# The selected-keys mixer: lower weight halves on another engine, and scaling ahead of maxima

## The chip, the cores and the metric

The kernel runs as one program on one core of one Trainium2 chip. The metric is the device time of one execution in microseconds; lower is better. The engines are named as in the profile: PE (TensorE matmul), PEld (its weight loads), DVE (VectorE), ACT (ScalarE), POOL (GpSimd) and SP (SyncE, which issues the weight loads).

## The reference, cut to what matters

Four layers run one after the other on 256 rows of width 1024: two of a first block (convolutions, attention, experts) and two of a second. The change touches one place, the mixer of the last layer (`_nsa`). It has 16 heads in 4 groups that share keys and values. Each head attends three times: to 15 compressed keys, to selected keys, and to a window of keys. At 256 rows the selection holds every earlier block and the window every earlier key, so both are causal attention over all keys, with different key projections:

```python
def _masked_softmax(s, mask):
    s = jnp.where(mask, s.astype(F32), -jnp.inf)
    m = jnp.max(s, axis=-1, keepdims=True)
    e = jnp.exp(s - m)
    l = jnp.sum(e, axis=-1, keepdims=True)
    p = e / jnp.where(l > 0, l, 1.0)

# selected keys, and the same with kw, vw for the window:
s = jnp.einsum('bghqd,bgqkd->bghqk', qc, kk) * ATTN_SCALE + bias
pr, _ = _masked_softmax(s, (dist >= 0)[:, :, None])
out = jnp.einsum('bghqk,bgqkd->bghqd', pr, vv)
# o = gate0 * o_cmp + gate1 * o_slc + gate2 * o_win, then o @ w_out
```

## The kernel before

**Weights.** Every dense product is made of three matmuls (`mm3`, L397 to L399) from a weight's higher and lower part. A weight tile of 1 MB has two halves of 128x1024. ACT rounds a half to its higher part (`wh`, L237). The lower part is the difference (`wl`, L248), made on DVE, or on POOL while the switch `on_pool` is set. `half()` and `tick()` do this up to three halves ahead of the matmuls. In the mixer `nsa_mix` the switch is set before the last two query units and cleared in the sixth tick of the output product.

**Attention by pairs.** Two heads with one kind of keys make a `Pair`; there are 16, four for each group: selected (0, 1), window (2, 3) and so on. A pair goes through these parts, and the words here are used below for pair n:
- scores(n): PE multiplies queries by keys (`two_heads`, L1375), each head into a bank of its own. For selected keys DVE also adds the bias of the compressed keys (L1790, "mask additions"). For the first window pair of a group DVE subtracts the compressed minima (L1819 to L1821), for the second it normalises the compressed weights (L1829 to L1837).
- M(n), maxima: four DVE instructions add the bias and take the extreme of each row (L1409). They read the banks of the scores, which are free after that.
- E(n): four exponentials on ACT with row sums (L1414).
- S(n), scaling: DVE inverts the sums, multiplies by the gate and scales the rows (L1419, L1421, four times L1424).
- T(n): PE turns the rows (L1431, six transposes into two banks) and ACT evicts them (`pT`, L1432).
- V(n): PE multiplies by the values (L1442, L1444). After a window pair ACT and DVE split the result for the output product (`yh`, L1447, and `yl`, L1448).

**Order.** Nothing is scheduled: each engine takes its instructions in the order in which the code is written. `step()` number i runs scores(i) and M(i) with E(i), then S(i-1), T(i-2), V(i-3) (L1770). Steps 0 and 1 lie in the two value units; step 1 falls into the matmuls of the third query unit. Steps 2, 3 and 4 follow closely, step 5 stands inside the fourth query unit, steps 6 to 10 follow closely again, and steps 11 to 18 are called one by one in the ticks of the output product `feat_out`, between groups of 24 weight matmuls. A query unit also has a norm: ACT squares (L1338), DVE reduces (L1340 to L1342), POOL takes a power (L1344), DVE scales (L1348, L1350), PE turns, and ACT and DVE write the result (L1365, L1366). PSUM has eight banks; `feat_out` holds four of them, and scores, transposes and values share the rest.

Of the kernel before, what the change touches and what calls it, by code (L numbers as in the profile page):

```python
# [70 lines left out]
def tile_kernel(ctx: ExitStack, tc: tile.TileContext, A, out, first=0, last=9):  # L71
# [120 lines left out]
    def pump(n=1000):  # L192
        while loaded[0] < len(items) and n:
            i = loaded[0]
            p = next((p for p in free if usable(p, i)), None)
            if p is None:
                return
            free.remove(p)
            t = pools[p].tile([128, 2048], F32, name="w", tag="w")
            v = items[i]  # L200
            a, b = v.shape[1], v.shape[2]
            Q.dma_start(t[:, :a * b].rearrange("p (a b) -> p a b", a=a), v)
            raw[i], where[i] = t, p
            loaded[0] += 1
            n -= 1
# [19 lines left out]
    on_pool = [False]  # L225
# [45 lines left out]
    def later(n, f):  # L271
        heapq.heappush(due, (now[0] + n, now[1], f))
        now[1] += 1
# [127 lines left out]
    def feat_unit(xh, xl, opening=False):  # L401

        ps = bank()
        for m in range(2):
            h, l = half()
            if opening and not m:
                for a, b in ((h, xh), (l, xh), (h, xl)):
                    for k in range(8):
                        T.matmul(ps[:, 0:256], a[:, k, :], b[:, k, :], start=a is h and b is xh and k == 0,
                                 stop=b is xl and k == 7)  # L410
                tick()
                continue
            for k in range(8):
                mm3(ps[:, m * 256:(m + 1) * 256], h[:, k, :], l[:, k, :], xh[:, k, :], xl[:, k, :], k == 0, k == 7)
            tick()
        return ps
# [889 lines left out]
    def feat_out(yh, yl, nxt):  # L1306

        pss = [bank() for _ in range(4)]

        def part(u, h, l, c0, ks):  # L1310
            for m in range(2):
                q = slice(c0 + m * 128, c0 + m * 128 + 128)
                for i, k in enumerate(ks):
                    mm3(pss[u][:, m * 256:(m + 1) * 256], h[:, i, q], l[:, i, q], yh[:, k, :], yl[:, k, :],
                        k == 0 and m == 0, k == 7, skip_group_check=True)
                if not m:
                    middle()
        for k in range(0, 8, 2):
            if k == 6:
                drain()  # L1320
            for j in range(2):
                h, l = half()
                for u in (2 * j, 2 * j + 1):
                    part(u, h, l, (u % 2) * 256, (k, k + 1))
                    if k == 6:
                        add_unit(u, pss[u], nxt)
                        if u == 2:
                            split_high(limit(here[0] + 2))
                if k < 6:
                    tick()  # L1330
        nxt(4)
# [61 lines left out]
    class Pair:  # L1393
# [6 lines left out]
            self.gate, self.values = gate, values  # L1400

        def a(self):
            banks = self.scores()
            m = sm.tile([128, 2, 2], F32, name="sM", bufs=3)
            l = self.l = sm.tile([128, 2, 2], F32, name="sL", bufs=3)
            s = self.s = self.pool.tile([128, 2, 384], F32, name="sS", bufs=3)
            for r in range(2):
                for c, (a, n) in enumerate(PARTS):
                    V.tensor_tensor_reduce(out=s[:, r, a:a + n], in0=banks[r][:, self.starts[c]:self.starts[c] + n],  # L1409
                                           in1=self.biases[r][:, 0:n], scale=1.0, scalar=3e38, op0=OP.add,  # L1410
                                           op1=OP.min, accum_out=m[:, r, c:c + 1])
            for r in range(2):
                for c, (a, n) in enumerate(PARTS):
                    S.activation(s[:, r, a:a + n], s[:, r, a:a + n], AF.Exp, scale=-1.0, bias=m[:, r, c:c + 1],  # L1414
                                 accum_out=l[:, r, c:c + 1])
# [210 lines left out]
    def nsa_mix(bp, sl, cur, nxt):  # L1626
        with tc.tile_pool(name="ns", bufs=1, reuse_waits="tile") as cp, \
# [138 lines left out]
            def step():  # L1766

                i = step.n
                step.n += 1
                for j, f in ((i, "a"), (i - 1, "b"), (i - 2, "c"), (i - 3, "d")):  # L1770
                    if 0 <= j < len(steps):
                        getattr(steps[j], f)()
            step.n = 0
# [93 lines left out]
            for j in range(2):  # L1867
                vals.append(scaled_values(cp, tok_unit(xh, xl), cur.r, f"val{j}"))
                later(1, step)
            on_pool[0] = True  # L1870
            for g in (2, 3):
                qs, turn_q = q_unit(g)
                step()
                step()
                plan(g, bias_of(g))
                qs()
                step()
                turn_q()
                if g == 2:
                    later(1, step)  # L1880
# [2 lines left out]
            nx = nxt()  # L1883
            for j in range(1, 9):
                later(j, step)
            later(6, lambda: on_pool.__setitem__(0, False))
            feat_out(yh, yl, nx.put)
            return nx

# [17 lines left out]
    def second_block():  # L1907
        nonlocal jdent, sm
        with tc.tile_pool(name="b2", bufs=1, reuse_waits="tile") as bp, tc.tile_pool(name="sm2", bufs=2) as sm:
# [32 lines left out]
            for i, base in ((0, 5), (1, 8)):  # L1942
                if base == 8 and s0 <= 7 <= last:
                    cur = nsa_mix(bp, sl, cur, nxt(7))
                if s0 <= base + 1 and last >= base:
                    with tc.tile_pool(name="ff", bufs=1, reuse_waits="tile") as cp, \
                            tc.tile_pool(name="ffw", bufs=2, reuse_waits="tile") as cw:
                        pl = Ple(cp, i) if last > base else None
                        if s0 <= base:
                            on_pool[0] = False  # L1950
                            cur = ffn(cp, cw, i, cur, nxt(base), [(12, pl.turn)] if pl else [])
                        else:
                            pl.turn()
                        if pl:
                            cur2 = []

                            def nx1():
                                cur2.append(nxt(base + 1)())
                                return cur2[0].put
                            ple(cp, cw, pl, cur, nx1)  # L1960
                            cur = cur2[0]
# [3 lines left out]
    if 7 in stage_half:  # L1965
        j = halves[stage_half[7]][0]
# [51 lines left out]
```

## Time and profile before

| what | value |
|---|---|
| median of 3 runs | 1919.6 us (1918.84 to 1921.35) |
| the profiled execution | 1918.91 us |
| its span in the trace | 1917.3 us |
| PE, PEld busy | 85%, 64% |
| DVE, ACT, POOL busy | 39%, 35%, 6% |
| selected-keys mixer, steps 0 to 18 | about 1585 to 1683 us of the span |

Busy shares are means over stages with different limits. Most of the span is spent on the experts' weights; the mixer in question is some 100 us of it, with POOL splits at L248 among its rows. A time in the rows is counted from the span's start, and "idle before <-" names what the engine waited for last.

### The profile page before, as it was taken

What the parts mean: (1) busy time and instruction counts of PE and PEld (TensorE: products, weight loads), DVE (VectorE), ACT (ScalarE), POOL (GpSimd) and SP (SyncE); (2) the same over time, 40 slices, a digit from 0 to 9 for tenths busy, and PEclk for the clock granted to TensorE, in tenths of its full rate; (3) what the DMA queues carried; (4) which work ended last, traced back from release to release, by engine and by line L of the source; (5) the groups of instructions that cost most, each with busy time, mean ns of one, the idle gap of its engine ahead of it and who ended that gap; (6) DMA issues with size and microseconds to landing.
All of it is one profiled execution on the core that took longest, in us unless ns stands there. A gap on an engine that the chain in (4) does not pass through costs nothing. (4 is left out here: it accounts for less than half of the span.)

```text
span 1917.3 us, 35268 instructions
## 1 busy us (share of the span) xinstructions
PE 1631.0 (85%) x15117; PEld 1228.9 (64%) x15117; DVE 738.6 (39%) x1503; ACT 676.8 (35%) x1297; POOL 122.0 (6%) x126
## 2 busy tenths in 40 slices
PE   8999667677679998767667669999999998999998
PEld 7875323233238985323224227999999996799998
DVE  5551000001005661001001005666656857666557
ACT  4422111111116643111111114655444645654445
POOL 0010000000001000000000002101000412210002
PEclk9999878777789999878778789999999998999999
DMA  9689999999999469999999998545555463145550
GB/s 295 239 306 416 419 418 418 420 419 418 417 406 360 162 257 396 418 419 419 418 419 419 417 419 272 173 138 172 190 194 177 143 202 100 56 156 196 183 176 23
DMA packets 236571, 559.07 MB, mean 292 GB/s; under 512 B 15563, under 2 KB 124938, under 8 KB 236408
## 3 DMA queue, kind: packets, MB, share of 16 engines
q1 hardware_dynamic: 226520, 551.59, 75.2%
q10 hardware_dynamic: 9264, 4.97, 0.9%
q8 instruction: 122, 2.00, 0.4%
q14 instruction: 41, 0.34, 0.0%
q0 software_dynamic: 624, 0.18, 0.0%
HBM read 555.55 MB, written 1.15 MB: 290 GB/s over the span
## 5 line engine op out<-in xcount | busy, mean ns | idle before, releaser
L904 PE MATMUL ps<-w,xg 128*32 128x256 f32 x4096 | 365.0, 496 | 233.3 <-DMA w<-in_expert_w_up_dram 232.1
L904 PEld LDWEIGHTS ps<-w,xg 128*32 128x32 f32 x4096 | 136.1, 132 | 444.2 <-DMA w<-in_expert_w_up_dram 264.1
L248 DVE TENSOR_TENSOR wl<-w,wh 128x1024 fp32r<-128x1024 f32 x255 | 310.1, 1228 | 171.6 <-ACT wh L237 167.4
L237 ACT ACTIVATE wh<-w 128x1024 fp32r<-128x1024 f32 x273 | 283.1, 1051 | 91.5 <-PE ps L398 60.3
L908 DVE TENSOR_TENSOR hs<-hs,ps 128x128 f32<-128x128 f32 x64 | 18.4, 288 | 632.4 <-ACT hs L907 632.4
L397 PE MATMUL ps<-xh,wh 128*128 128x256 f32 (+1 forms) x840 | 237.1, 282 | 0.0
L399 PE MATMUL ps<-xh,wl 128*128 128x256 f32 (+1 forms) x840 | 236.3, 281 | 0.8 <-DVE wl L248 0.8
L398 PE MATMUL ps<-xl,wh 128*128 128x256 f32 (+1 forms) x840 | 236.6, 282 | 0.3 <-DVE xl L1229 0.3
L907 ACT ACTIVATE hs<-ps 128x128 f32<-128x128 f32 x64 | 17.8, 277 | 591.8 <-PE ps L904 587.2
L399 PEld LDWEIGHTS ps<-xh,wl 128*128 128x128 f32 (+1 forms) x840 | 159.2, 190 | 1.2 <-DVE wl L248 1.2
L398 PEld LDWEIGHTS ps<-xl,wh 128*128 128x128 f32 (+1 forms) x840 | 159.2, 190 | 1.1 <-DVE xl L1229 1.1
L397 PEld LDWEIGHTS ps<-xh,wh 128*128 128x128 f32 (+1 forms) x840 | 159.3, 190 | 0.0
L926 PE MATMUL ps<-w,ht 128*32 128x256 f32 x2048 | 142.2, 425 | 0.4 <-DMA w<-in_expert_w_down_dram 0.4
L933 ACT ACTIVATE y<-ps 32x256 f32<-32x256 f32 x256 | 95.8, 374 | 118.5 <-PE ps L926 111.6
L926 PEld LDWEIGHTS ps<-w,ht 128*32 128x32 f32 x2048 | 73.6, 127 | 67.6 <-issue 33.9
L399 PE MATMUL ps<-wh,xl 128*128 128x256 f32 x352 | 100.9, 287 | 4.5 <-DVE xl L1229 4.5
L397 PE MATMUL ps<-wh,xh 128*128 128x256 f32 x352 | 103.1, 293 | 1.5 <-ACT xh L1226 1.5
L248 POOL TENSOR_TENSOR wl<-w,wh 128x1024 fp32r<-128x1024 f32 x18 | 43.4, 2416 | 942.3 <-ACT wh L237 463.4
L398 PE MATMUL ps<-wl,xh 128*128 128x256 f32 x352 | 100.6, 286 | 0.0
L398 PE MATMUL ps<-al,wh 128*128 128x256 f32 x352 | 99.1, 281 | 0.0
L397 PE MATMUL ps<-ah,wh 128*128 128x256 f32 x352 | 99.1, 281 | 0.0
L399 PE MATMUL ps<-ah,wl 128*128 128x256 f32 x352 | 99.0, 281 | 0.0
(400 smaller groups left out, 2756.3 us busy)
## 6 DMA issues: line engine op xcount, KB each, us to landing
w<-in_expert_w_up_dram SPq DMA_DIRECT2D x256, 1024.0 KB
w<-in_expert_w_down_dram SPq DMA_DIRECT2D x128, 1024.0 KB
w<-in_w_ffn_gate_dram SPq DMA_DIRECT2D x22, 1024.0 KB
w<-in_w_ffn_up_dram SPq DMA_DIRECT2D x22, 1024.0 KB
w<-in_w_ffn_down_dram SPq DMA_DIRECT2D x22, 1024.0 KB
w<-in_odd_w_qkv_dram SPq DMA_DIRECT2D x12, 1024.0 KB
w<-in_w_in_ab_dram SPq DMA_DIRECT2D x12, 1024.0 KB
w<-in_w_in_nsa_dram SPq DMA_DIRECT2D x10, 1024.0 KB
```

The costliest lines, as they stand in the source:

```text
L237: S.activation(hv, src, AF.Copy)
L248: eng.tensor_tensor(out=lv, in0=src, in1=hv.bitcast(F32), op=OP.subtract)
L397: T.matmul(ps, lh, rh, start=start, stop=False, **kw)
L398: T.matmul(ps, lh, rl, start=False, stop=False, **kw)
L399: T.matmul(ps, ll, rh, start=False, stop=stop, **kw)
L904: T.matmul(pu[32 * j:32 * j + 32, 0:256], r, w[:, kk, :, j, :], start=k == 0, stop=k == 7)
L907: S.activation(hs, pu[:, 0:128], AF.Silu)
L908: V.tensor_tensor(out=hs, in0=hs, in1=pu[:, 128:256], op=OP.mult)
L926: T.matmul(pd[32 * c:32 * c + 32, 0:256], hts[e][:, 32 * j:32 * j + 32], w[:, jj, c * 256:(c + 1) * 256], start=j == 0, stop=j == 3)
L933: S.activation(y4s[q][32 * ee:32 * ee + 32, c * 256:(c + 1) * 256], pd[32 * c:32 * c + 32, 0:256], AF.Copy)
```

## The change

Two things are changed. `on_pool` is no longer set in `nsa_mix`, so that the nine lower halves that POOL made there are made on DVE, at the place in DVE's order at which the code asks for them. And `Pair.a` is cut in two, scores (`a0`) and maxima with exponentials (`a1`); `step()` now runs scores(i), S(i-1), M(i) with E(i), T(i-2), V(i-3). The other mixer that uses `Pair` calls `a`, which runs both parts at once as before.

```diff
         def a(self):
-            banks = self.scores()
+            self.a0()
+            self.a1()
+
+        def a0(self):
+            self.banks = self.scores()
+
+        def a1(self):
+            banks = self.banks
             m = sm.tile([128, 2, 2], F32, name="sM", bufs=3)
...
                 i = step.n
                 step.n += 1
-                for j, f in ((i, "a"), (i - 1, "b"), (i - 2, "c"), (i - 3, "d")):
+                for j, f in ((i, "a0"), (i - 1, "b"), (i, "a1"), (i - 2, "c"), (i - 3, "d")):
...
-            on_pool[0] = True
             for g in (2, 3):
...
-            later(6, lambda: on_pool.__setitem__(0, False))
             feat_out(yh, yl, nx.put)
```

On PE, ACT and SP every instruction keeps its place. DVE's order between M(10) and M(11), the last closely following steps, was this (sS_14238 belongs to pair 9; the next row is the first of M(11)):

```order
L1419 RECIPROCAL sL_14237<-sL_14237 128x4
L1421 TENSOR_TENSOR sL_14237<-sL_14237,gate_12972 128x4
L1424 TENSOR_SCALAR sS_14238<-sS_14238,sL_14237 128x128
L1424 TENSOR_SCALAR sS_14238<-sS_14238,sL_14237 128x256
L1424 TENSOR_SCALAR sS_14238<-sS_14238,sL_14237 128x128
L1424 TENSOR_SCALAR sS_14238<-sS_14238,sL_14237 128x256
L1448 TENSOR_TENSOR yl_12967<-ps_14211,yh_12966 128x256
L1829 TENSOR_REDUCE cl_14350<-scm_14180 128x8
L1830 TENSOR_SCALAR cl_14350<-cl_14350 128x8
L1831 RECIPROCAL cl_14350<-cl_14350 128x8
L1833 TENSOR_TENSOR cl_14350<-cl_14350,gate_12972 128x4 x2
L1837 TENSOR_TENSOR pc0_12973<-scm_14180,cl_14350 128x4x16 x2
```

and is now, again up to the first row of M(11) (sS_14291 belongs to pair 10; lines are 7 higher):

```order
L1455 TENSOR_TENSOR yl_12967<-ps_14211,yh_12966 128x256
L1836 TENSOR_REDUCE cl_14350<-scm_14180 128x8
L1837 TENSOR_SCALAR cl_14350<-cl_14350 128x8
L1838 RECIPROCAL cl_14350<-cl_14350 128x8
L1840 TENSOR_TENSOR cl_14350<-cl_14350,gate_12972 128x4 x2
L1844 TENSOR_TENSOR pc0_12973<-scm_14180,cl_14350 128x4x16 x2
L1426 RECIPROCAL sL_14290<-sL_14290 128x4
L1428 TENSOR_TENSOR sL_14290<-sL_14290,gate_12972 128x4
L1431 TENSOR_SCALAR sS_14291<-sS_14291,sL_14290 128x128
L1431 TENSOR_SCALAR sS_14291<-sS_14291,sL_14290 128x256
L1431 TENSOR_SCALAR sS_14291<-sS_14291,sL_14290 128x128
L1431 TENSOR_SCALAR sS_14291<-sS_14291,sL_14290 128x256
```

The scaling that stands between two blocks of maxima was that of pair 9, directly behind M(10); it is now that of pair 10, at the end, directly ahead of M(11).

DVE between M(11) and M(12), in the output product, before (the first row ends M(11), the last begins M(12)):

```order
L1409 ISA sM_14364 128x1
L1419 RECIPROCAL sL_14284<-sL_14284 128x4
L1421 TENSOR_TENSOR sL_14284<-sL_14284,gate_12972 128x4
L1424 TENSOR_SCALAR sS_14285<-sS_14285,sL_14284 128x128
L1424 TENSOR_SCALAR sS_14285<-sS_14285,sL_14284 128x256
L1424 TENSOR_SCALAR sS_14285<-sS_14285,sL_14284 128x128
L1424 TENSOR_SCALAR sS_14285<-sS_14285,sL_14284 128x256
L1790 TENSOR_TENSOR scm_14433<-ps_14427,cb_12968 128x32
L1790 TENSOR_TENSOR scm_14433<-ps_14428,cb_12968 128x32
L1409 ISA sS_14438,sM_14436<-ps_14427,bias_14168 128x128
```

and now:

```order
L1416 ISA sM_14370 128x1
L248 TENSOR_TENSOR wl_14398<-w_13334,wh_14397 128x1024
L1797 TENSOR_TENSOR scm_14433<-ps_14427,cb_12968 128x32
L1797 TENSOR_TENSOR scm_14433<-ps_14428,cb_12968 128x32
L1426 RECIPROCAL sL_14371<-sL_14371 128x4
L1428 TENSOR_TENSOR sL_14371<-sL_14371,gate_12972 128x4
L1431 TENSOR_SCALAR sS_14372<-sS_14372,sL_14371 128x128
L1431 TENSOR_SCALAR sS_14372<-sS_14372,sL_14371 128x256
L1431 TENSOR_SCALAR sS_14372<-sS_14372,sL_14371 128x128
L1431 TENSOR_SCALAR sS_14372<-sS_14372,sL_14371 128x256
L1416 ISA sS_14444,sM_14442<-ps_14427,bias_14168 128x128
```

A lower half came to stand between the two blocks, and the scaling (of pair 11, no longer of pair 10) behind the mask additions.

## Rows read from the trace of the kernel before

**Rows 1.** A stretch: us; busy of PE, PEld, DVE, ACT, POOL (instructions); granted clock; DMA
```profile
1626.00:1632.20 6.20, 6.10 (x28) 4.18 (x28) 5.28 (x28) 4.00 (x15) 0.00 (x0) 0.50 0.08 21
```

**Rows 2.** PE's waits from 1584 to 1692 us: total us, times, longest
```profile
PE ps L1431 <- DVE sS L1424: 8.4, 3, 5.3
PE ps L1431 <- DVE sM L1409: 1.9, 3, 1.0
```

**Rows 3.** ACT's waits in the same stretch
```profile
ACT sS L1414 <- DVE sM L1409: 22.7, 12, 3.4
```

**Rows 4.** Timeline of DVE, start and duration in us: M(2), S(1), normalising, M(3)
```profile
1601.50 0.28 DVE L1409 CUSTOM_DVE_ANT_0 sS<-ps,bias 128x128 f32<-128x128 f32 x1
...
1602.61 0.17 DVE L1419 RECIPROCAL sL<-sL 128x4 f32<-128x4 f32 x1
...
1603.94 0.28 DVE L1829 TENSOR_REDUCE cl<-scm 128x8 f32<-128x128 f32 x1
...
1605.17 0.28 DVE L1409 CUSTOM_DVE_ANT_0 sS<-ps,bias 128x128 f32<-128x128 f32 x1
```

**Rows 5.** Groups of DVE by shape, 1500 to 1700 us: busy, mean ns, idle before
```profile
L248 DVE TENSOR_TENSOR wl<-w,wh 128x1024 fp32r<-128x1024 f32 x26 | 31.7, 1231 | 15.8 <-ACT wh L237 12.6 <-POOL ssum L1242 3.1
```

**Rows 6.** Timeline of DVE, M(10) to M(11)
```profile
1641.06 0.28 DVE L1409 CUSTOM_DVE_ANT_0 sS<-ps,bias 128x128 f32<-128x128 f32 x1
...
1644.30 0.42 DVE L1448 TENSOR_TENSOR yl<-ps,yh 128x256 fp32r<-128x256 f32 x1 [0.71 <-ACT yh L1447]
...
1645.86 0.28 DVE L1409 CUSTOM_DVE_ANT_0 sS<-ps,bias 128x128 f32<-128x128 f32 x1
```

**Rows 7.** Timeline of ACT behind E(10)
```profile
1643.16 0.84 ACT L1432 ACTIVATE pT<-ps 128x384 f32<-128x384 f32 x2
1643.90 0.36 ACT L1447 ACTIVATE yh<-ps 128x256 fp32r<-128x256 f32 x1
```

**Rows 8.** Timeline of POOL: lower halves
```profile
1618.85 4.67 POOL L248 TENSOR_TENSOR wl<-w,wh 128x1024 fp32r<-128x1024 f32 x2 [16.27 <-ACT wh L237]
...
1669.46 2.39 POOL L248 TENSOR_TENSOR wl<-w,wh 128x1024 fp32r<-128x1024 f32 x1 [4.34 <-ACT wh L237]
```

**Rows 9.** Timeline of DVE: L1342 once, L1833 at two times
```profile
1621.27 2.28 DVE L1342 TENSOR_SCALAR hss<-hss 128x8 f32<-128x8 f32 x1
...
1628.52 0.24 DVE L1833 TENSOR_TENSOR cl<-cl,gate 128x4 f32<-128x4 f32 x2
...
1669.56 2.38 DVE L1833 TENSOR_TENSOR cl<-cl,gate 128x4 f32<-128x4 f32 x2
```

**Rows 10.** Timeline of DVE: M(5), the norm's reduction, M(6), M(7), M(8)
```profile
1614.61 0.28 DVE L1409 CUSTOM_DVE_ANT_0 sS<-ps,bias 128x128 f32<-128x128 f32 x1
...
1620.23 0.69 DVE L1340 TENSOR_REDUCE hss<-hsq 128x8 f32<-128x512 f32 x1 [1.95 <-ACT hsq L1338]
...
1624.18 0.28 DVE L1409 CUSTOM_DVE_ANT_0 sS<-ps,bias 128x128 f32<-128x128 f32 x1
...
1628.99 0.28 DVE L1409 CUSTOM_DVE_ANT_0 sS<-ps,bias 128x128 f32<-128x128 f32 x1
...
1632.53 0.28 DVE L1409 CUSTOM_DVE_ANT_0 sS<-ps,bias 128x128 f32<-128x128 f32 x1
```

**Rows 11.** Timeline of ACT: two higher halves ahead of the norm's square
```profile
1617.71 2.00 ACT L237 ACTIVATE wh<-w 128x1024 fp32r<-128x1024 f32 x2
```

**Rows 12.** DVE in the output product: mask additions, M(12), M(13), M(14), M(15)
```profile
1650.71 0.32 DVE L1790 TENSOR_TENSOR scm<-ps,cb 128x32 f32<-128x32 f32 x2 [2.32 <-PE ps L1375]
1650.94 0.28 DVE L1409 CUSTOM_DVE_ANT_0 sS<-ps,bias 128x128 f32<-128x128 f32 x1
...
1658.04 0.28 DVE L1409 CUSTOM_DVE_ANT_0 sS<-ps,bias 128x128 f32<-128x128 f32 x1
...
1665.22 0.29 DVE L1409 CUSTOM_DVE_ANT_0 sS<-ps,bias 128x128 f32<-128x128 f32 x1 [2.33 <-PE ps L1375]
...
1672.49 0.29 DVE L1409 CUSTOM_DVE_ANT_0 sS<-ps,bias 128x128 f32<-128x128 f32 x1 [0.22 <-PE ps L1375]
```

## The prediction

> **What bounds the kernel now.** I read the stretches first, then the waits of PE and ACT in the mixer, then the timelines of DVE, ACT and POOL there. Outside the mixer nothing moves. In it PE waits almost only for the transposes: 8.4 us for scaled rows and 1.9 us for maxima, whose end frees the banks that the transposes write [rows 2]. ACT waits 22.7 us, in 12 pieces, for maxima [rows 3]. So where steps follow closely, neither PE nor a busy engine sets the pace, but a loop between DVE and ACT. It can be read whole between M(10) and M(11) [rows 6, 7]: M(10) starts at 1641.06, the exponentials hold ACT until 1643.16, the two evictions until 1643.90, the split of the last result ends at 1644.26, DVE takes it up at 1644.30 and then normalises, and M(11) starts at 1645.86. That is 4.80 us, and in it the scaling S(9), which stands right behind M(10), costs nothing: DVE would wait anyway, and still sits idle 0.71 us behind it [rows 6]. DVE's own prices stand between M(2) and M(3) [rows 4]: maxima 1602.61 - 1601.50 = 1.11 us, scaling 1603.94 - 1602.61 = 1.33 us, normalising 1.23 us. The exponentials end some 2.2 us after their maxima start (1641.06 to 1643.16, and a tenth for the last sum).
>
> **The change: scaling ahead of maxima.** M(i) now stands behind S(i-1), which needs all sums of E(i-1). The loop therefore becomes maxima, exponentials, whatever DVE has ahead of the scaling, scaling, maxima. The 1.33 us that lay beside ACT's work move onto the loop, unless DVE has at least 2.2 - 1.11 = 1.1 us of work of its own that needs nothing late from ACT. I go step by step.
> - M(2) to M(3) has the normalising (1.23 us), so 1.11 + 1.23 + 1.33 = 3.67 us both ways [rows 4]: 0. M(7) to M(8) was 1632.53 - 1628.99 = 3.54 us [rows 10], so that the query norm's scaling and the mask additions in it take 1.1 us beside maxima and scaling; they just fill the gap, and I take +0.05, for M(3) to M(4) too.
> - M(6) to M(7), M(9) to M(10) and M(10) to M(11) have an instruction in front of the scaling that waits for the `yh` that ACT makes behind the exponentials and evictions; M(8) to M(9) has the write of turned queries, which waits for ACT in the same place. All four are the loop of rows 6 and 7 and pay in full: 4 x 1.33 = +5.3.
> - Up to M(6): M(1) and M(5) come behind mask additions that wait for PE and then pay 1.33 us each, but idle time of DVE ahead of M(5) takes the first of them back. I put M(5) at +1.4, with 0 to +2.7 as its bounds.
>
> Together M(11) starts 1.4 + 0.1 + 5.3 = 6.8 us later. The early S has no reader that gains: T(n) writes a bank that M(n+1) must have read, so transposes wait for both blocks, 2.44 us in either order.
>
> **The change: lower halves on DVE.** Nine halves of 2.4 us leave POOL [rows 8] and nine of 1.23 us come to DVE [rows 5], 11 us of work on an engine that is idle part of the time. Four of them stand in two pairs ahead of a query norm. In the second of these, M(5) to M(6), the norm's reduction started at 1620.23, when ACT had finished two higher halves (from 1617.71) and the square [rows 10, 11]. Now the first lower half can begin at about 1618.75 and the second ends at 1621.1: the reduction moves 0.85 us back. But POOL's pair no longer runs beside it, and L1342, an instruction over 8 elements a row that took 2.28 us under it [rows 8, 9], gives some 2.1 back (L1833, of a like size, lost 2.38 - 0.24 = 2.14). With the 1.33 us of S(5) that is +0.85 - 2.1 + 1.33 = +0.1, so M(6) keeps the +1.4.
>
> The other five come in the ticks of the output product. Each waits for its higher half, which ACT makes behind exponentials, evictions and the split of a result; behind it on DVE stand mask additions, scaling and maxima, and behind these maxima wait E on ACT and, for the bank, T on PE.
> - M(11) to M(12) was 1650.94 - 1645.86 = 5.08 us [rows 6, 12]. Now: exponentials 2.1, evictions 0.74, higher half 1.0 [rows 11], lower half 1.23 [rows 5], mask additions 1650.94 - 1650.71 = 0.23, scaling 1.33, in all 6.63: +1.6. PE comes no earlier, for it waits for M(11) and for the evictions too.
> - M(12) to M(13), 7.10 us [rows 12], is PE's path: transposes behind M(12), values, 24 weight matmuls, scores. It stays, but scaling now lies between the mask additions and the maxima: +1.3.
> - M(13) to M(14), 7.18 us: the loop with a split (0.36 [rows 7]), a higher and a lower half, the minima (an estimate of 0.7, between the mask additions and the normalising) and scaling adds up to about 7.5, and PE may add to it with the values that the split waits for: +0.6, with 0.3 as its lower bound. The 2.33 us that DVE was idle there [rows 12] are used up.
> - M(14) to M(15), 7.27 us, with the normalising in it and without the 2.1 us that L1833 lost under POOL [rows 8, 9]: 2.1 + 0.74 + 0.36 + 1.0 + 1.23 + 1.23 + 1.33 = 8.0, +0.7.
> - Behind M(15) a group of weight matmuls covers E(15) and S(15); without that cover they would cost 1.3.
>
> Sum: 6.8 + 1.6 + 1.3 + 0.6 + 0.7 = +11.0 us. What POOL's power instruction gains by standing alone is covered by M(2) and M(3). SP's order and the weights' loads are as before; no wait of PE in the mixer is for a load.
>
> **The clock.** Behind PE's two longest waits (most of the 8.4 us) the granted clock is 0.50, 1.2 GHz, as in the 6.2 us behind the second of them [rows 1]. It cost little, since the loop and not PE set the pace: M(6) to M(7), most of it at 0.50, took 1628.99 - 1624.18 = 4.81 us [rows 10], as long as M(10) to M(11) at full clock. Such a stretch of about 6 us over weight matmuls would cost 3. PE will wait more, also in the output product: I take +1; if both stretches go, it is at best -1, with two more of them over weight matmuls +6.
>
> The profiled execution took 1918.91 us, so +12 gives 1930.9. The median of the runs shown is 0.7 higher: **1931.5**.
>
> **The rivals.**
> - *The blocked instructions decide, and it gets faster.* The two long waits of PE are for S(1) and S(5), each behind a norm in which DVE stood blocked 2.1 us beside POOL [rows 2, 9]. If the two lower halves hide under ACT's higher halves, and scaling first lets the transposes go earlier, PE gains 2 x 2.1 = 4.2: 1915.4, some us less if the low clock goes too. The Trainium skill, SBUF — State Buffer, section Who interferes with whom, backs the blocking: a VectorE instruction with two SBUF inputs and a GpSimd instruction that reads SBUF exclude each other for a whole instruction. For L1833 the trace agrees, 2.38 us for two against 0.24 [rows 9]; by that page alone the change could only gain. It decides as soon as M(i) has more than 1.33 us of slack, and 22.7 us of ACT's waiting for maxima [rows 3] say that it has none.
> - *The output product absorbs the delay.* DVE's idle times ahead of M(12) and M(14), 2.32 and 2.33 us [rows 12], swallow part of the 6.8 us, and only the bank waits of T(10) and T(11) grow by 1.3 each: about +5, 1924.6. Against it: these idle times are waits for PE, and PE is late with the rest.
> - *The clock.* If PE's new waits bring two more stretches at 0.50 over weight matmuls, it is +6 in place of +1: 1936.5 and more.
> - *Nothing shows.* All is hidden, the change is then within 0.2%: 1919.6. It needs slack in steps 6 to 11, where rows 6 show none.
>
> **How the numbers follow.** Chances: the forecast 0.60 (alone 1927 to 1936), faster by the blocking 0.08, absorbed 0.14, clock 0.11, nothing 0.07. The range of 8 in 10 runs from 1923.5 to 1937.5; it leaves out the faster case, no change, and half of the clock's. Within 0.2% (3.8 us, about what a measurement of this kernel can tell from no change) lie the case of nothing and a little of the absorbed one, 0.09; slower 0.83; faster 0.08.
>
> **What would show it.** In the trace of the changed kernel, M(6) to M(7) and M(10) to M(11) should be about 6.1 us apart, M(7) to M(8) still 3.6, M(11) to M(12) about 6.6. PE's waits on the transposes should be for maxima, no longer for scaled rows; L1342 and L1833 should be short throughout; and the mixer should end 11 to 12 us later. The forecast is wrong if those distances stay at 4.8 us, if PE's waits shrink, or if the distances grow as said and the end does not move.

## The result and the profile after

The changed kernel takes 1936.2 us (median of 4 runs, 1934.46 to 1936.96) beside 1920.1 us of the kernel before on the same chip: a ratio of 1.0078 [1.0066, 1.009], 16 us slower. Five further runs on another occasion gave 1936.1 us and 1.0077 [1.0064, 1.0091]. The forecast was 1931.5 us in a range of 1923.5 to 1937.5: the direction and the mechanism held, and the size came out 4.7 us too small, 1.3 us inside the upper end of the range.

The profiled execution took 1936.68 us, 17.8 more than the one of before. By the starts of the maxima, 2.5 us of that stand ahead of M(0) (1588.67 against 1586.20), 15.8 between M(0) and M(15), and 0.5 us are won back behind. What is ahead of M(0) is scatter: the code is the same there, and in the executions of the experiments below M(0) starts anywhere between 1586.8 and 1591.9, the latest in kernels that are fast. So the change costs 15.8 us inside the mixer, and this is what has to be explained. Lines of the changed kernel have numbers 7 higher there: maxima L1416, exponentials L1421, scaling L1426, L1428 and L1431, transposes L1438, evictions L1439.

The waits in the changed kernel from 1584 to 1708 us (what waits and for whom; total us, times, longest), to be read against [rows 2, 3]:

```profile
ACT sS L1421 <- DVE sM L1416: 38.2, 15, 5.1
...
PE ps L1438 <- DVE sM L1416: 10.0, 7, 3.3
...
PE ps L1438 <- DVE sS L1431: 4.1, 1, 4.1
```

TensorE's transposes now wait 10.0 us for maxima, where it was 1.9, and 4.1 us for scaled rows, where it was 8.4; that one piece is T(1), behind the first norm. ACT waits 38.2 us for maxima instead of 22.7: the 15.5 us more are nearly the whole loss.

The timeline of DVE in the changed kernel, first of each group of four maxima, M(6) to M(8) and M(10), M(11), to be read against [rows 6, 10]:

```profile
1629.62 0.28 DVE L1416 CUSTOM_DVE_ANT_0 sS<-ps,bias 128x128 f32<-128x128 f32 x1
...
1635.75 0.28 DVE L1416 CUSTOM_DVE_ANT_0 sS<-ps,bias 128x128 f32<-128x128 f32 x1
...
1639.31 0.29 DVE L1416 CUSTOM_DVE_ANT_0 sS<-ps,bias 128x128 f32<-128x128 f32 x1
...
1650.50 0.28 DVE L1416 CUSTOM_DVE_ANT_0 sS<-ps,bias 128x128 f32<-128x128 f32 x1
...
1653.73 0.42 DVE L1455 TENSOR_TENSOR yl<-ps,yh 128x256 fp32r<-128x256 f32 x1 [2.04 <-ACT yh L1454]
...
1655.71 1.01 DVE L1431 TENSOR_SCALAR sS<-sS,sL 128x128 f32<-128x128 f32 x4
1656.63 0.28 DVE L1416 CUSTOM_DVE_ANT_0 sS<-ps,bias 128x128 f32<-128x128 f32 x1
```

M(6) to M(7) is 6.13 us (4.81 before), M(10) to M(11) 6.13 (4.80), M(7) to M(8) 3.56 (3.54). Between M(10) and M(11) the idle time of DVE ahead of `yl` has grown from 0.71 us [rows 6] to 2.04, by the 1.33 us of scaling that were done there, and the scaling stands behind it, right ahead of M(11). The last run of weight matmuls of the mixer starts at 1700.96 us, where it was 1682.67: 18.3 us later with the 2.5 us ahead of M(0), and so 15.8 by the mixer, not 11 to 12.

The two instructions that were held beside POOL are short now, as is seen in the second norm and in the output product (DVE, same view), to be read against [rows 9]:

```profile
1624.29 2.36 DVE L248 TENSOR_TENSOR wl<-w,wh 128x1024 fp32r<-128x1024 f32 x2 [0.52 <-ACT wh L237]
...
1627.48 0.17 DVE L1342 TENSOR_SCALAR hss<-hss 128x8 f32<-128x8 f32 x1
...
1688.99 0.24 DVE L1840 TENSOR_TENSOR cl<-cl,gate 128x4 f32<-128x4 f32 x2
```

### The profile page after: what moved, and what is told of

It is laid out like the page before. It is cut to its first block, busy times and chain, and to the rows that moved or that the text cites. A ratio compares the mean times of both kernels' runs of the same rounds, so it can differ in the third digit from the quotient of the medians.

```text
span 1935.1 us, 35255 instructions
## 1 busy us (share of the span) xinstructions
PE 1644.8 (85%) x15117; PEld 1236.7 (64%) x15117; DVE 742.4 (38%) x1512; ACT 677.2 (35%) x1297; POOL 101.0 (5%) x117
## 5 line engine op out<-in xcount | busy, mean ns | idle before, releaser
L248 DVE TENSOR_TENSOR wl<-w,wh 128x1024 fp32r<-128x1024 f32 x264 | 321.0, 1228 | 181.6 <-ACT wh L237 181.5
L397 PE MATMUL ps<-w,wh 128*128 128x256 f32 x272 | 78.5, 289 | 0.0
```

Of the source, the lines that this page charges most:

```text
L248: eng.tensor_tensor(out=lv, in0=src, in1=hv.bitcast(F32), op=OP.subtract)
L397: T.matmul(ps, lh, rh, start=start, stop=False, **kw)
```

## The experiments

All kernels come from the kernel before or the changed one with one thing altered. The table has the distances between starts of maxima in us, read from the DVE timeline of each, the median of the kernel, and its ratio to the kernel before, timed beside it on the same chip. M(0) to M(6) holds the two norms, M(6) to M(11) the steps that follow closely, M(11) to M(15) the output product. Each row of distances is one execution; the column M(0) to M(6) differs by 1.3 us between two kernels that are the same there (lower halves alone, 34.32, and new order from step 11, 35.62), for which the account of the prediction gives the reason.

| kernel | M0 to M6 | M6 to M11 | M11 to M15 | median us | ratio [95%] |
|---|---|---|---|---|---|
| before | 37.98 | 21.68 | 26.63 | 1920.1 | |
| changed | 40.95 | 27.01 | 34.17 | 1936.2 | 1.0078 [1.0066, 1.009] |
| lower halves alone | 34.32 | 21.67 | 26.82 | 1919.1 | 0.9988 [0.9979, 0.9997] |
| order alone | 43.01 | 27.01 | 33.44 | 1937.9 | 1.0093 [1.0077, 1.0108] |
| changed, new order to step 10 | 41.06 | 25.71 | 27.79 | 1930.3 | 1.005 [1.0036, 1.0063] |
| changed, new order from step 11 | 35.62 | 23.03 | 34.09 | 1926.7 | 1.003 [1.0018, 1.0043] |
| changed, half the scaling | 38.22 | 24.73 | 32.60 | 1931.4 | 1.0051 [1.0036, 1.0066] |
| before, half the scaling | 37.83 | 21.23 | 26.60 | 1921.0 | 0.9994 [0.9985, 1.0004] |
| changed, wait filled | 40.93 | 27.20 | 30.78 | 1933.0 | 1.0061 [1.0045, 1.0076] |
| halves alone, mask additions late | 34.35 | 21.24 | 26.89 | 1917.7 | 0.9982 [0.9973, 0.9991] |

### The two parts, each alone

The lower halves alone (the changed kernel with the order of the steps set back):

```diff
-                for j, f in ((i, "a0"), (i - 1, "b"), (i, "a1"), (i - 2, "c"), (i - 3, "d")):
+                for j, f in ((i, "a"), (i - 1, "b"), (i - 2, "c"), (i - 3, "d")):
```

> The nine lower halves of the mixer on the DVE, the steps' order as before. Theory (the order makes most of the loss): M(6) to M(11) as before, 21.7 us; the blocked sums of the norms (2.28 us) and the blocked compressed product (2.38 us) are gone, about -2 us by M(6) and a little more at the last pairs, against +1.23 us for each lower half that stands on the DVE's chain; in all -2 to +4 us, 1917.5 to 1924. Rival 1 (the lower halves make most of it): +8 us or more. Rival 2 (the two parts are cheap alone and dear together): under +2 us here and under +4 us for the order alone.

The order alone (the changed kernel with the switch to POOL put back):

```diff
+            on_pool[0] = True
             for g in (2, 3):
...
+            later(6, lambda: on_pool.__setitem__(0, False))
             feat_out(yh, yl, nx.put)
```

> The new order of the steps, the nine lower halves on GpSimd as before. Theory: M(6) to M(7), M(8) to M(9), M(9) to M(10) and M(10) to M(11) longer by 1.33 us each (one pair's scaling), M(4) to M(5) too, M(11) to M(12) by 1.3 to 1.5; TensorE waits on maxima where it waited on scaled rows; the sums of the norms still take 2.3 us beside GpSimd. In all +9 to +13 us, 1929 to 1933. Rival 1 (the lower halves make most of it): +3 to +6 us, with the intervals in the output product as before. Rival 2: under +4 us.

The parts have opposite signs. From M(0) to M(15) the lower halves alone take 82.81 us against 86.29 before, 3.5 us less, and the kernel is 0.12% faster; the order alone takes 103.46 us, 17.2 us more. This is more than the 9 to 13 us expected: M(0) to M(6) pays 5.0 us, since nothing there is won back, and the output product 6.8, with a group of weight matmuls of 3.87 us in it (below). M(6) to M(11) is the same 27.01 us with either engine for the lower halves: there the loss is the order's alone. The first rival (the lower halves make most of it) falls, and so does the second: the order alone costs more than the whole change. What the lower halves win looks smaller under the new order, 103.46 - 102.12 = 1.3 us in place of 3.5. The norms don't differ in that: M(1) to M(2) and M(5) to M(6) are 1.4 us shorter each with the halves on DVE, in either order. Most of the difference lies in M(4) to M(5), which falls from 5.91 to 5.18 us in the old order and rises from 6.56 to 7.24 in the new; this is the distance that also differs by 1.3 us between two kernels that are the same there. So 2.8 us of the gain are shown, and the rest is not.

The win lies in the norms. Groups of DVE in the output of the order alone, from 1590 to 1700 us (busy us, mean ns of one, idle before):

```profile
L1342 DVE TENSOR_SCALAR hss<-hss 128x8 f32<-128x8 f32 x2 | 4.5, 2270 | 0.1
...
L1840 DVE TENSOR_TENSOR cl<-cl,gate 128x4 f32<-128x4 f32 x8 | 3.1, 428 | 0.1
```

and the same groups with the lower halves alone on DVE:

```profile
L1840 DVE TENSOR_TENSOR cl<-cl,gate 128x4 f32<-128x4 f32 x8 | 0.9, 160 | 0.1
...
L1342 DVE TENSOR_SCALAR hss<-hss 128x8 f32<-128x8 f32 x2 | 0.3, 172 | 0.1
```

L1342 takes 2.27 us beside POOL's halves and 0.17 without them. The Trainium skill, SBUF — State Buffer, section Who interferes with whom, says that besides instructions with two SBUF inputs the two-port form of `tensor_scalar` is locked out while GpSimd holds the shared ports. L1342 is a `tensor_scalar`, and its 2.27 and 0.17 us agree, though no row shows in which form it ran. M(5) to M(6), which holds one of the two, is 8.19 us with the lower halves alone, 9.57 before, 10.89 with the order alone and 9.51 with both: -1.38 and +1.32 cancel.

### Where the order costs it

The new order in a part of the steps only; the first kernel uses it up to step 10, the second (with `i > 10` in place of `i < 11`) from step 11 on:

```diff
-                for j, f in ((i, "a0"), (i - 1, "b"), (i, "a1"), (i - 2, "c"), (i - 3, "d")):
+                for j, f in (((i, "a0"), (i - 1, "b"), (i, "a1"), (i - 2, "c"), (i - 3, "d")) if i < 11 else
+                             ((i, "a"), (i - 1, "b"), (i - 2, "c"), (i - 3, "d"))):
```

> As the changed kernel, but from step 11 on (the output product) in the order of before. Theory: M(0) to M(11) as in the changed kernel, 68 us against 59.7; behind M(11) as in the kernel with the lower halves alone. In all +7 to +11 us, 1927 to 1931. Rival (the loss lies in the output product): under +4 us.

> As the changed kernel, but up to step 10 in the order of before; the new order only in the output product. Theory: M(0) to M(10) as with the lower halves alone; from M(11) on as in the changed kernel, 4 to 7 us over before. In all +3 to +9 us, 1923 to 1929. Rival (the loss lies in the output product): +12 us or more.

Both ranges held, on the ratio 1.005 and 1.003. Against the lower halves alone, from M(0) to M(15), the early steps cost 94.56 - 82.81 = 11.8 us and the late ones 92.74 - 82.81 = 9.9. Counted in their own steps these are 10.8 us up to M(10) and 8.6 from M(10) on, together 19.4, which is what the new order costs on the whole with the lower halves on DVE (102.12 - 82.81 = 19.3). The rest lies where the two kernels have the old order: 1.0 us in M(12) to M(13) of the first, behind a TensorE wait of 2.0 us and with a granted clock of 0.86 in the weight matmuls that follow (3.23 us in place of 2.86), and 1.3 in M(4) to M(5) of the second. Neither stretch has the loss to itself, and each rival (all of it in the output product, or nearly none) falls. The product was dearer than the 4 to 7 us that I gave it.

### Is it the scaling's length?

Half of the multiplications of S(n) are left out in the mixer, once in the changed kernel and once in the kernel before:

```diff
         def b(self):
...
-            for r in range(2):
+            for r in range(2 if self.values.__name__ == "values" else 1):
                 for c, (a, n) in enumerate(PARTS):
```

> The changed kernel without the scaling of the second head of each pair of the mixer (two of the four L1431 multiplications, 0.46 to 0.5 us), so that its output isn't the reference's. Theory (each step pays the whole scaling that stands ahead of its maxima): M(6) to M(7), M(8) to M(9), M(9) to M(10) and M(10) to M(11) each shorter by about 0.5 us than in the changed kernel (5.6, 5.1, 5.1, 5.6 us), M(7) to M(8) the same; in all 4 to 7 us under the changed kernel, 1929 to 1932. Rival (the loss is a fixed cost of the new order, such as a later release of a bank, and not the scaling's length): the intervals as in the changed kernel within 0.1 us, 1935 to 1937.

> The kernel before without the same two multiplications (its output isn't the reference's either). Theory (there the scaling stands behind the maxima, in time that the maxima don't need): M(6) to M(7) 4.8, M(8) to M(9) 4.2, M(9) to M(10) 4.3, M(10) to M(11) 4.8 us as before, within 0.15; in all 0 to -2 us. Rival (the DVE bounds these steps in either order): each interval shorter by 0.4 to 0.5 us, 4 to 6 us in all.

The first starts of maxima M(6), M(7) and M(8) in the changed kernel with half the scaling (DVE timeline; two scaling instructions are left ahead of each):

```profile
1627.72 0.28 DVE L1416 CUSTOM_DVE_ANT_0 sS<-ps,bias 128x128 f32<-128x128 f32 x1
...
1632.93 0.55 DVE L1431 TENSOR_SCALAR sS<-sS,sL 128x128 f32<-128x128 f32 x2
1633.40 0.28 DVE L1416 CUSTOM_DVE_ANT_0 sS<-ps,bias 128x128 f32<-128x128 f32 x1
...
1636.03 0.55 DVE L1431 TENSOR_SCALAR sS<-sS,sL 128x128 f32<-128x128 f32 x2
1636.50 0.28 DVE L1416 CUSTOM_DVE_ANT_0 sS<-ps,bias 128x128 f32<-128x128 f32 x1
```

M(6) to M(7) falls from 6.13 to 5.68 us, M(8) to M(9) from 5.56 to 5.10, M(9) to M(10) from 5.63 to 5.17 and M(10) to M(11) from 6.13 to 5.68: 0.45 to 0.46 us each, the length of the two instructions taken away. In the order of before the same four distances stay at 4.81, 4.23, 4.30 and 4.81 us. So with the new order each of these steps pays the scaling in full, and with the old order it is free. The expectation was wrong on one distance: M(7) to M(8) doesn't stay the same without half the scaling, it falls by 0.46 us in both kernels (3.55 to 3.10 and 3.53 to 3.08). There DVE's own work was the limit before, scaling included, which is why the new order doesn't lengthen it.

### The clock in the output product

In the product the forecast distances were nearly met where no weight matmuls follow a long wait: M(11) to M(12) is 6.61 us. M(12) to M(13) and M(13) to M(14) are 9.48 and 10.18 us, 1.1 and 2.4 over what was forecast. The stretches of the changed kernel show where (us; busy of PE, PEld, DVE, ACT, POOL with instructions; granted clock; DMA share, GB/s):

```profile
1660.00:1664.00 4.00, 0.69 (x5) 0.32 (x4) 3.38 (x14) 0.95 (x4) 0.00 (x0) 1.00 0.20 49
1664.00:1668.00 4.00, 3.94 (x21) 3.23 (x22) 0.44 (x5) 3.51 (x11) 0.00 (x0) 0.60 0.52 213
...
1676.50:1681.70 5.20, 5.20 (x26) 5.13 (x24) 3.57 (x11) 1.64 (x3) 0.00 (x0) 0.50 0.21 64
1682.00:1700.00 18.00, 16.88 (x135) 12.69 (x136) 10.06 (x39) 10.64 (x30) 0.00 (x0) 1.00 0.26 86
```

and the timeline of TensorE (start, duration, idle before) has the waits and the matmuls behind them:

```profile
1660.15 0.55 PE L1438 MATMUL ps<-jdent,sS 128*128 128x128 f32 x3
1664.03 0.52 PE L1438 MATMUL ps<-jdent,sS 128*128 128x128 f32 x3 [3.33 <-DVE sM L1416]
...
1666.24 0.56 PE L397 MATMUL ps<-yh,wh 128*128 128x256 f32 x1
...
1669.95 0.28 PE L399 MATMUL ps<-yh,wl 128*128 128x256 f32 x1
...
1673.50 1.08 PE L1438 MATMUL ps<-jdent,sS 128*128 128x128 f32 x6 [2.37 <-DVE sM L1416]
...
1676.57 0.58 PE L397 MATMUL ps<-yh,wh 128*128 128x256 f32 x1
...
1681.64 0.38 PE L399 MATMUL ps<-yh,wl 128*128 128x256 f32 x1
```

T(10)'s second head waits 3.33 us for the bank that M(12) reads, T(11) waits 2.37 us for M(13). Behind each, the granted clock is 0.60 and 0.50 on average, that is 1.2 GHz for a part or all of the stretch. The group of 24 weight matmuls behind T(11) goes from 1676.57 to 1681.64 in starts, 5.07 us, the one behind T(10) from 1666.24 to 1669.95, 3.71 us; in the kernel before such a group took 2.86. Together 3.1 us. To try it, the first wait is filled with transposes whose result nothing reads:

```diff
                     T.transpose(pt[:, i * 128:(i + 1) * 128], self.s[:, r, a:a + 128], jdent)
+                for i in range(self.fill if r == 0 else 0):
+                    T.transpose(pt[:, 384:512], self.s[:, r, 0:128], jdent)
                 S.activation(o[:, r, :], pt[:, 0:384], AF.Copy)
...
+                        steps[j].fill = 16 * (j == 10)
                         getattr(steps[j], f)()
```

> The changed kernel with 16 more transposes (some 2.2 us of TensorE) between T(10)'s two heads, in the 3.6 us in which TensorE waits there, into columns that nothing reads. Theory (the wait lowers the granted clock behind it): the 24 weight matmuls behind T(10) take 2.86 us, not 3.71, and M(12) to M(13) falls from 9.48 by 0.5 to 0.9 us; the 24 behind T(11), whose wait of 2.65 us isn't filled, still take 3.5 us or more. In all 0 to -1.5 us against the changed kernel, 1934.5 to 1936.5. Rival (these matmuls are slow because they wait for their split weights): they take 3.7 us as before, and the total stays or rises by up to 1 us.

Stretches of the kernel with the filled wait; its two groups of 24 matmuls start at 1664.31 and 1673.09:

```profile
1661.30:1665.00 3.70, 2.27 (x19) 1.77 (x20) 1.39 (x10) 3.02 (x12) 0.00 (x0) 1.00 0.68 267
1664.30:1667.20 2.90, 2.90 (x26) 2.90 (x25) 1.23 (x1) 1.46 (x3) 0.00 (x0) 1.00 0.01 4
...
1673.00:1676.00 3.00, 3.00 (x26) 2.92 (x24) 1.85 (x3) 1.33 (x2) 0.00 (x0) 1.00 0.00 0
```

With the added work the product is 3.4 us shorter: M(11) to M(15) falls from 34.17 to 30.78 us, and both groups take 2.85 us at full clock. That the matmuls wait for their split weights, the rival, is thereby out. My expectation was wrong in one point: I held the second group to stay slow, since its wait isn't filled, and it is fast as well, behind a wait of 2.38 us, as long as in the changed kernel (2.37). So the stretch gained more than the 0 to 1.5 us expected. To see whether this is more than one execution's luck, the changed kernel and this one ran once more, side by side:

> The changed kernel itself, as the mate on one chip of the next kernel. 1.0066 to 1.009 of the kernel before; the 24 weight matmuls behind T(10) and those behind T(11) together 8 to 9 us, with stretches at a granted clock of 0.50 over them.

> The changed kernel with 16 transposes in TensorE's wait between T(10)'s two heads, in five rounds beside the changed kernel. Theory (the clock behind that wait costs what the trace showed, 34.17 - 30.78 = 3.4 us from M(11) to M(15)): 2.5 to 4 us under the changed kernel on this chip, both groups of 24 matmuls at 2.86 us again. Rival (the low stretch comes and goes from execution to execution, whatever is filled): within 1 us of the changed kernel's median, and here or there a slow group in the profile.

The profiles repeat to about a tenth of a us: 34.19 us without and 30.77 with the filled wait, groups of 3.81 and 5.08 us against 2.83 and 2.86. Granted clock of two equal stretches, first without the filling:

```profile
1660.00:1668.00 8.00, 4.51 (x26) 3.73 (x25) 4.42 (x18) 3.94 (x12) 0.00 (x0) 0.79 0.36 131
...
1674.00:1684.00 10.00, 9.74 (x55) 7.69 (x56) 4.77 (x19) 4.10 (x14) 0.00 (x0) 0.66 0.35 107
```

and with it:

```profile
1660.00:1668.00 8.00, 5.96 (x51) 5.17 (x50) 4.21 (x18) 4.36 (x13) 0.00 (x0) 1.00 0.40 131
...
1674.00:1684.00 10.00, 8.93 (x71) 6.58 (x66) 5.50 (x21) 5.97 (x17) 0.00 (x0) 1.00 0.36 105
```

The medians are 1936.1 and 1933.2 us, 2.9 apart as expected, though their intervals against the kernel before (1.0077 [1.0064, 1.0091] and 1.0066 [1.0052, 1.0081]) overlap: the 3.4 us are shown by the four traces, not by the times alone. That the filling sped up the first group is shown; that it sped up the second is not. The kernel with the order alone has the same second wait, nothing filled, a slow group behind the first wait (3.87 us) and a fast one behind the second (2.86 us):

```profile
1666.23 0.87 PE L1438 MATMUL ps<-jdent,sS 128*128 128x128 f32 x3 [3.76 <-DVE sM L1416]
...
1676.27 1.08 PE L1438 MATMUL ps<-jdent,sS 128*128 128x128 f32 x6 [2.37 <-DVE sM L1416]
```

```profile
1668.80:1673.00 4.20, 4.20 (x28) 4.07 (x26) 0.00 (x0) 1.33 (x2) 2.36 (x1) 0.71 0.04 15
...
1678.60:1682.00 3.40, 3.40 (x28) 3.21 (x28) 2.71 (x6) 1.64 (x3) 1.82 (x1) 1.00 0.00 0
```

In the four other profiles with the new order in the product and neither wait filled the second group is slow (4.65 to 5.08 us). What decides it stays open; a filling of the second wait alone wasn't tried.

### A better version

If what stands ahead of the maxima is paid for, it should pay to move something else behind them. The kernel with the lower halves alone, with the mask additions of a selected pair behind its maxima:

```diff
                                            op1=OP.min, accum_out=m[:, r, c:c + 1])
+            if self.late is not None:
+                self.late(banks)
             for r in range(2):
...
+                    return bk
+
+                def masked(m, bk):
                     for r, sc in enumerate(bk):
...
-                    return bk
...
+                    if b == "s":
+                        steps[-1].late = lambda bk, m=m: masked(m, bk)
```

> The kernel with the lower halves on the DVE and the steps' order of before, with the two additions to the compressed scores (0.23 us each) behind the maxima of their pair. Theory (what stands ahead of the maxima on the DVE is paid for, what stands behind is free): each of the eight pairs of selected keys takes its maxima 0.2 to 0.46 us earlier after its scores; where the maxima end a TensorE wait or an exponential's wait that counts, that is won; 0 to -3 us against the kernel with the lower halves alone, 1916 to 1919. Rival (the steps are bound by TensorE's own order, and the maxima have slack there): within 1 us of it, 1918 to 1920.

It takes 1917.7 us, 0.9982 [0.9973, 0.9991] of the kernel before, and M(0) to M(15) is 82.48 us, 0.3 less than with the lower halves alone (0.5 with M(0) itself, which no longer has its additions ahead of it). It is faster than the kernel before and the changed one. What I overlooked is that the additions read the banks of the scores too, so that behind the maxima they hold these banks longer. The transposes now wait 2.5 us for them, where with the lower halves alone they wait 1.9 us for maxima:

```profile
PE ps L1442 <- DVE scm L1804: 2.5, 2, 1.5
```

Against the lower halves alone (0.9988 [0.9979, 0.9997]) the times can't tell the difference, nor between my theory and its rival.

## Why the prediction was right, and where it was short

The forecast was +12 us, the mixer's steps measured +15.8. (Its total should read 1931.6 us, since 1918.91 + 12 + 0.69 is that and not 1931.5.) By its own terms:

- **The steps that follow closely, +5.3 and 0.05.** Measured +5.33 from M(6) to M(11), with 1.32, 1.33, 1.33 and 1.32 us at the four distances named and 0.02 at M(7) to M(8). That it is the scaling's length is shown by leaving half of it out: 0.45 us less in each, and nothing in the order of before.
- **Up to M(6), +1.4 with 0 to +2.7.** Measured +2.97, over the upper bound: a mis-sized term. M(0) to M(1) grew by 1.13 us, M(3) to M(4) by 0.59 instead of 0.05, M(4) to M(5) by 1.34. The step that failed is "idle time of DVE ahead of M(5) takes the first of them back". DVE's last wait ahead of M(5) is for scores(5), first before and then in the changed kernel:

```profile
1614.38 0.32 DVE L1790 TENSOR_TENSOR scm<-ps,cb 128x32 f32<-128x32 f32 x2 [1.53 <-PE ps L1375]
```

```profile
1618.54 0.32 DVE L1797 TENSOR_TENSOR scm<-ps,cb 128x32 f32<-128x32 f32 x2 [1.53 <-PE ps L1375]
```

  It is 1.53 us in both, and takes nothing back, because TensorE comes later too. Scores(4) and scores(5) on TensorE before:

```profile
1606.37 1.76 PE L1375 MATMUL ps<-kst,qt 64*128 64x272 f32 x8
...
1613.38 0.97 PE L1375 MATMUL ps<-kst,qt 64*128 64x272 f32 x8
```

  and in the changed kernel, with the second head of T(1) and V(0) ahead of them:

```profile
1605.74 0.90 PE L1438 MATMUL ps<-jdent,sS 128*128 128x128 f32 x3 [0.30 <-DVE sM L1416]
1607.67 1.49 PE L1449 MATMUL ps<-pT,val 128*64 128x256 f32 x4 [1.02 <-ACT pT L1439]
...
1609.51 1.76 PE L1375 MATMUL ps<-kst,qt 64*128 64x272 f32 x8
...
1617.54 0.97 PE L1375 MATMUL ps<-kst,qt 64*128 64x272 f32 x8
```

  T(1)'s second head waits for M(2). V(0) waits for an eviction that ACT makes behind E(2), and so behind M(2) again. From V(0) to scores(5) TensorE has no gap. Counted from M(0), M(2) starts 1.08 us later than before, scores(4) 0.67 and scores(5) 1.69; with the 1.33 us of S(4) this is the +3.0 at M(5). The 1.02 us in between are the clock, which stays low longer (first before, then changed):

```profile
1608.30:1614.40 6.10, 6.10 (x53) 5.27 (x53) 3.37 (x19) 3.24 (x12) 0.00 (x0) 1.00 0.25 71
```

```profile
1608.30:1612.70 4.40, 4.40 (x24) 2.95 (x21) 3.78 (x22) 2.61 (x10) 0.00 (x0) 0.50 0.26 70
```

  How long it stays low there is not settled by the order: in two kernels that are the same up to step 10, scores(5) start 6.28 us (lower halves alone) and 7.57 us (new order from step 11) after scores(4). TensorE has no gap in either, and in the 3 us from scores(4) on the granted clock is 0.98 in the first and 0.50 in the second. The write of `qt`, the other idle time of DVE ahead of M(5), is done half a us before TensorE reaches scores(5) in both kernels and decides nothing. In M(3) to M(4) DVE idles 0.51 us ahead of the mask additions for scores(4), which are late by the same path, where the forecast had its work just filling the gap.
- **The norms, +0.85 - 2.1 + 1.33 = +0.1.** M(5) to M(6) measured -0.06; alone, the parts are -1.38 for the lower halves (-1.25 by these terms) and +1.32 for the order.
- **The output product, +1.6, +1.3, +0.6 and +0.7.** Measured +1.53, +2.38, +3.00 and +0.62, 7.5 us in place of 4.2. With the wait filled, and so at full clock, the same distances are 6.62, 8.43, 7.85 and 7.89 us: +1.54, +1.33, +0.67 and +0.62, together +4.2. The working of rows was right, and the rest is the clock.
- **The clock, +1 with -1 to +6.** The two groups of matmuls take 3.1 us more, and with the first wait filled, both groups at full clock, the product is 3.4 us shorter: the second mis-sized term, 2.4 us too small. The low stretches [rows 1] were known and priced at 3 us over weight matmuls, and TensorE's waits on M(12) and M(13) follow from the forecast's own sum; taking the bound from the rows there, and not a third of it, would have been right. Two low stretches over weight matmuls are what the clock's rival said, but only the second lies wholly over its group, so that they cost 3 us and not 6. The measured 1936.2 us are nearer to that rival's 1936.5 than to the forecast's 1931.5, but only 4.4 of the 15.8 us are clock (3.4 here and 1.0 up to M(5)); the other 11.4 are about the 11.0 that the forecast had without the clock.

Together 2.97 + 5.33 + 4.16 + 3.39 = 15.85 us, the 15.8 measured. The missing 3.8 us are 1.5 up to M(6), 1.0 of it clock as well, 2.4 of clock in the output product, and nothing of the rest. Of the rivals, the one that made it faster named a true gain: without the held instructions the two norms take 2.8 us less in the old order. It fell on its condition, 1.33 us of slack ahead of the maxima. The output product did not absorb anything.

## What to carry to other kernels

When an instruction is moved ahead of the one on which the next engine waits, ask what ended the engine's idle time at the old place: if it is work that the moved instruction delays, its whole length is paid in every turn of the loop, whatever the busy shares say (DVE was at 39%). Idle time is a cushion only where its end doesn't hang on the delayed chain; that has to be followed back one engine further, here from DVE's wait for scores(5) through TensorE and an eviction on ACT behind E(2) to M(2). And a change of two parts should be timed in its parts, since here one was a gain of 2.8 us or more in the mixer, hidden under a loss of 17.

## What the runs showed of the hardware

That added work can shorten a stretch was new to me: 16 idle transposes, 1.6 us between the first start and the last, in a wait of 3.3 us left the granted clock at 1.00 behind it, in two of two profiles, and the group of 24 weight matmuls behind it took 2.83 to 2.84 us in place of 3.71 to 3.81. And a wait of 2.4 us was followed by 1.2 GHz in the changed kernel, in two profiles, but not in the two in which the wait before it was filled, nor in the kernel with the order alone, where nothing was filled. So the price of a wait isn't told by its length alone, and the same code can cost 1.3 us more by the clock in one execution than in another (M(4) to M(5), 5.18 and 6.49 us).
